# The second tile of a split GELU-multiply: loaded in two transfers of four rows, computed in two steps of four rows

## The chip, the cores and the metric

The kernel runs on one core of a Trainium2 chip. The metric is device time in microseconds of one execution, the median of three runs. The engines that take part are ScalarE (ACT), which computes the GELU and issues most stores, VectorE (DVE), which multiplies, SyncE (SP), which issues all loads and the last stores, and the core's 16 DMA engines, which move the data.

## The reference

```python
x = np.random.randn(32, 512, 2048).astype(np.float32)

def reference(x):
    half_dim = x.shape[-1] // 2
    x1, x2 = x[..., :half_dim], x[..., half_dim:]
    gelu_x1 = 0.5 * x1 * (1 + erf(x1 / np.sqrt(2)))
    return (gelu_x1 * x2).astype(np.float32)
```

The input has 16384 rows of 2048 float32 (134.2 MB); the output has 16384 rows of 1024 (67.1 MB).

## The kernel before

The rows are cut into 16 tiles. A tile is 128 partitions of R = 8 rows each, and the 8 rows of one partition lie next to each other in memory: 64 KB per partition in, 32 KB out, so 8.39 MB in and 4.19 MB out for a tile. There are two input buffers (`x0`, `x1`) and two output buffers (`o0`, `o1`); tile i uses number i % 2 of each.

Nothing is scheduled by a planner. The order on each engine is the order in which the Python loop issues it, and all waits are written by hand:

- `load` (L49) issues a load on SyncE; `store` (L56) lets the issuing engine wait until VectorE has done all multiplies so far (`mul_done`) and then issues the store.
- Before the loop, tile 0 is loaded in two halves of four rows (semaphores `first[0]` and `first[1]`), and tile 1 in one transfer of eight rows (L69; semaphore `ready[1]`). A 4 KB load of scrap is issued on ScalarE.
- In the loop (from L75), each tile is computed in steps. Tiles 0 and 15 take rows (0,2), (2,4), (4,8); all others rows (0,5), (5,8) (L79). A step is a GELU on ScalarE (L87) from the first half of each row into the output buffer, and then a multiply on VectorE (L95) of that with the second half of each row, in place.
- ScalarE waits at a tile's first step for `ready[k]`, which counts both the load of this tile and the store of the tile two before it, whose output buffer it takes over.
- Tile 0 is stored by two half stores on ScalarE; tiles 1 to 13 by one store each on ScalarE; tile 14 by one, and tile 15 by two half stores, on SyncE.
- After tile i, SyncE waits for its last multiply and issues the load of tile i + 2 into the buffer that has come free. So up to two loads can stand in SyncE's DMA ring, and up to two stores in ScalarE's.

At the end ScalarE, VectorE and SyncE clear the semaphores (L119 to L125), and SyncE waits for the last three stores.

Of the kernel before, what the change touches and what calls it, by code (L numbers as in the profile page):

```python
# [1 line left out]

# [4 lines left out]

GELU = mybir.ActivationFunctionType.Gelu


@with_exitstack
def kernel(
    ctx: ExitStack,
    tc: tile.TileContext,
    x: bass.AP,
    out: bass.AP,
):
    nc = tc.nc
    P = nc.NUM_PARTITIONS

    x_flat = x.flatten_outer_dims()
    out_flat = out.flatten_outer_dims()
    n_rows, dim = x_flat.shape
    half = dim // 2

    R = 8
    x_t = x_flat.rearrange("(n p r) d -> n p r d", p=P, r=R)
    o_t = out_flat.rearrange("(n p r) d -> n p r d", p=P, r=R)
    n_tiles = x_t.shape[0]
    x_bufs = [nc.alloc_sbuf_tensor(f"x{k}_tile", [P, R, dim], x.dtype) for k in range(2)]  # L30
    o_bufs = [nc.alloc_sbuf_tensor(f"o{k}_tile", [P, R, half], out.dtype) for k in range(2)]

    first = [nc.alloc_semaphore(f"first{j}") for j in range(2)]
    ready = [nc.alloc_semaphore(f"ready{k}") for k in range(2)]
    gelu_done = nc.alloc_semaphore("gelu_done")
    mul_done = nc.alloc_semaphore("mul_done")
    tail_stored = nc.alloc_semaphore("tail_stored")
    opened = nc.alloc_semaphore("opened")  # L40
    scrap = nc.alloc_sbuf_tensor("scrap_tile", [8, 128], x.dtype)
    n = {sem.name: 0 for sem in [*first, *ready, gelu_done, mul_done, tail_stored, opened]}

    def counted(ins, sem, by):
        ins.then_inc(sem, by)
        n[sem.name] += by

    def load(i, rows, sem):
        ins = nc.sync.dma_start(out=x_bufs[i % 2][:, rows, :], in_=x_t[i][:, rows, :])  # L49
        counted(ins, sem, 16)  # L50
        return ins

    def store(queue, i, rows, sem):
        queue.wait_ge(mul_done, n[mul_done.name])
        counted(
            queue.dma_start(out=o_t[i][:, rows, :], in_=o_bufs[i % 2][:, rows, :]), sem, 16  # L56
        )

    opening = nc.scalar.dma_start(out=scrap[:, :], in_=x_t[0][:8, 0, :128])
    counted(opening, opened, 16)
    for ins in (
        opening,
        load(0, slice(0, 4), first[0]),
        load(0, slice(4, 8), first[1]),
        load(1, slice(0, 8), ready[1]),  # L69
    ):  # L70
        tc.no_tile_sem_insts.add(ins.ins.name)
    tc.close()
    tc.compile()  # L73

    for i in range(n_tiles):  # L75
        k = i % 2
        last = i == n_tiles - 1
        pieces = i == 0 or last
        steps = ((0, 2), (2, 4), (4, 8)) if pieces else ((0, 5), (5, 8))  # L79
        for lo, hi in steps:  # L80
            rows = slice(lo, hi)
            if i == 0 and lo % 4 == 0:
                nc.scalar.wait_ge(first[lo // 4], 16)
            elif lo == 0:
                nc.scalar.wait_ge(ready[k], n[ready[k].name])
            counted(
                nc.scalar.activation(  # L87
                    out=o_bufs[k][:, rows, :], in_=x_bufs[k][:, rows, :half], func=GELU
                ),
                gelu_done,  # L90
                1,
            )
            nc.vector.wait_ge(gelu_done, n[gelu_done.name])
            counted(
                nc.vector.tensor_mul(  # L95
                    out=o_bufs[k][:, rows, :],
                    in0=o_bufs[k][:, rows, :],
                    in1=x_bufs[k][:, rows, half:],
                ),
                mul_done,  # L100
                1,
            )
            if pieces and hi % 4 == 0:
                if last:
                    store(nc.sync, i, slice(hi - 4, hi), tail_stored)
                else:
                    store(nc.scalar, i, slice(hi - 4, hi), ready[k])
        if not pieces:
            if i == n_tiles - 2:
                store(nc.sync, i, slice(0, R), tail_stored)  # L110
            else:
                store(nc.scalar, i, slice(0, R), ready[k])
        if i + 2 < n_tiles:
            nc.sync.wait_ge(mul_done, n[mul_done.name])
            load(i + 2, slice(0, R), ready[k])


    nc.scalar.wait_ge(opened, 16)
    nc.scalar.drain()  # L119
    for sem in (*first, *ready, opened):  # L120
        nc.scalar.sem_clear(sem)
    nc.vector.drain()
    nc.vector.sem_clear(gelu_done)
    nc.sync.sem_clear(mul_done)
    nc.sync.wait_ge(tail_stored, n[tail_stored.name]).then_inc(  # L125
        tail_stored, -n[tail_stored.name]
    )


# [1 line left out]
_INS = ['x']  # L131
_OUTS = [((32, 512, 1024), 'float32')]


# [23 lines left out]
```

## Time and profile before

| what | value |
|---|---|
| time, median of 3 runs | 469.3 us (469.29 to 469.43) |
| span of the profiled execution | 467.8 us |
| VectorE busy | 140.5 us, 34 multiplies |
| ScalarE busy | 115.5 us, 34 GELUs and a table load |
| bytes moved by DMA | 201.34 MB, 430 GB/s over the span |

The span runs from the first to the last instruction of one profiled execution. The profiled execution's own time isn't listed apart from its span; the three runs lie 1.5 us above it, and that much is taken for what lies around the span. In the profile's rows a window's DMA share and GB/s book a packet where it starts, so that short windows go above and below the true rate; long ones are exact.

### The profile page before, as it was taken

The page shows a single profiled execution, that of the slowest core. Times are in us where ns is not written, and L with a number is a line of the kernel's source. Part 1 is how long each engine was busy: PE and PEld are TensorE (multiplying, and loading weights), DVE is VectorE, ACT ScalarE, POOL GpSimd, SP SyncE. Part 2 cuts the span into 40 slices and gives each one's busy share as a digit, 9 for nine tenths or more (in the row PEclk, how much of TensorE's full clock was granted, in tenths as well). Part 3 has the DMA queues.
Part 4 walks back from the last instruction along what each step waited for, and adds up shares of the span by engine and source line. Part 5 has one row for each costly group of instructions (what it writes and reads, how often), then busy time and mean ns, then how long its engine had stood idle before and what let it go on. Part 6 is the DMA issues. An engine that isn't in the chain of part 4 may idle for free.

```text
span 467.8 us, 154 instructions
## 1 busy us (share of the span) xinstructions
DVE 140.5 (30%) x34; ACT 115.5 (25%) x35; POOL 0.2 (0%) x4
## 2 busy tenths in 40 slices
DVE  0330515207051060511606115060150702507043
ACT  1320606041060410604105050050501506014060
POOL 0000000000000000000000000000000000000000
DMA  8999999999999999999999999999999999999988
GB/s 359 448 448 448 398 406 496 403 403 448 459 437 403 440 412 493 403 403 448 487 409 403 445 406 493 403 403 448 493 403 403 448 426 471 403 426 426 493 384 379
DMA packets 5057, 201.34 MB, mean 430 GB/s; under 512 B 568, under 2 KB 576, under 8 KB 576
## 3 DMA queue, kind: packets, MB, share of 16 engines
q1 hardware_dynamic: 2880, 142.61, 70.6%
q10 hardware_dynamic: 2176, 58.73, 29.1%
q14 instruction: 1, 0.01, 0.0%
HBM read 134.22 MB, written 67.11 MB: 430 GB/s over the span
## 4 chain that ended last, share of the span: by engine, by line
DMA 76%; DVE 14%; ACT 8%; ACTq 0%; SPq 0%; issue 0%
DMA out_dram<-o_tile 66%; DVE o_tile L95 14%; DMA x_tile<-in_x_dram 10%; ACT o_tile L87 8%; ACTq L119 0%; SPq L49 0%
## 5 line engine op out<-in xcount | busy, mean ns | idle before, releaser
L95 DVE TENSOR_TENSOR o_tile<-o_tile,x_tile 128x5120 f32<-128x5120 f32 (+3 forms) x34 | 140.5, 4171 | 319.7 <-ACT o_tile L87 319.7
L87 ACT ACTIVATE o_tile<-x_tile 128x5120 f32<-128x5120 f32 (+3 forms) x34 | 114.3, 3407 | 337.3 <-DMA out_dram<-o_tile 301.8
L87 ACT ACT_TABLE_LOAD x1 | 1.3, 1283 | 2.9 <-PEq L73 2.9
L142 POOL MEMSET const-bfloat16-1.0<- 128x1 bf16 x1 | 0.1, 102 | 0.0
L142 POOL MEMSET const-uint8-127<- 128x1 uint8 x1 | 0.1, 101 | 0.0
L142 POOL MEMSET const-float32-0.0<- 128x1 f32 x1 | 0.1, 99 | 0.2 <-issue 0.2
L142 POOL MEMSET const-float32-1.0<- 128x1 f32 x1 | 0.1, 98 | 0.0
## 6 DMA issues: line engine op xcount, KB each, us to landing
out_dram<-o_tile ACTq DMA_DIRECT2D x13, 4096.0 KB, 44.7
x_tile<-in_x_dram SPq DMA_DIRECT2D x2, 4096.0 KB, 16.7
out_dram<-o_tile ACTq DMA_DIRECT2D x2, 2048.0 KB, 34.4
out_dram<-o_tile SPq DMA_DIRECT2D x1, 4096.0 KB, 25.2
out_dram<-o_tile SPq DMA_DIRECT2D x2, 2048.0 KB, 7.8
x_tile<-in_x_dram SPq DMA_DIRECT2D x15, 44.4
scrap_tile<-in_x_dram ACTq DMA_DIRECT2D x1, 4.0 KB
```

Source lines behind the costliest of these rows:

```text
L87: nc.scalar.activation(out=o_bufs[k][:, rows, :], in_=x_bufs[k][:, rows, :half], func=GELU),
L95: nc.vector.tensor_mul(out=o_bufs[k][:, rows, :], in0=o_bufs[k][:, rows, :], in1=x_bufs[k][:, rows, half:],),
L142: nc = _bacc.Bacc("TRN2", target_bir_lowering=False, num_devices=1)
```

## The change

Tile 1 is loaded by two transfers, rows 0 to 4 and rows 4 to 8, each with a semaphore of its own (`ready[1]` and the new `second`). Both stand in SyncE's ring behind the two halves of tile 0, as the one transfer did. Tile 1 is computed in steps (0,4) and (4,8) instead of (0,5) and (5,8); its second GELU waits for `second`. Its store is still one transfer of eight rows after both steps. One more semaphore is cleared at the end. All other tiles are as they were.

```diff
+    second = nc.alloc_semaphore("second")
...
         load(0, slice(4, 8), first[1]),
-        load(1, slice(0, 8), ready[1]),
+        load(1, slice(0, 4), ready[1]),
+        load(1, slice(4, 8), second),
     ):
...
         steps = ((0, 2), (2, 4), (4, 8)) if pieces else ((0, 5), (5, 8))
+        if i == 1:
+            steps = ((0, 4), (4, 8))
         for lo, hi in steps:
             rows = slice(lo, hi)
             if i == 0 and lo % 4 == 0:
                 nc.scalar.wait_ge(first[lo // 4], 16)
+            elif i == 1 and lo == 4:
+                nc.scalar.wait_ge(second, 16)
             elif lo == 0:
                 nc.scalar.wait_ge(ready[k], n[ready[k].name])
...
-    for sem in (*first, *ready, opened):
+    for sem in (*first, *ready, opened, second):
         nc.scalar.sem_clear(sem)
```

More of the change, by code (lines that the diff above doesn't have):

```diff
@@ L40 @@
     opened = nc.alloc_semaphore("opened")
+    second = nc.alloc_semaphore("second")
     scrap = nc.alloc_sbuf_tensor("scrap_tile", [8, 128], x.dtype)
-    n = {sem.name: 0 for sem in [*first, *ready, gelu_done, mul_done, tail_stored, opened]}
+    n = {sem.name: 0 for sem in [*first, *ready, gelu_done, mul_done, tail_stored, opened, second]}
     def counted(ins, sem, by):
```

## The prediction

> **What bounds the kernel now.** I read the page's DMA rows first, because both engines are idle for most of the span (VectorE 30% busy, ScalarE 25%).
>
> ```profile
> span 467.8 us, 154 instructions
> DMA packets 5057, 201.34 MB, mean 430 GB/s; under 512 B 568, under 2 KB 576, under 8 KB 576
> q1 hardware_dynamic: 2880, 142.61, 70.6%
> q10 hardware_dynamic: 2176, 58.73, 29.1%
> ```
>
> q1 is SyncE's ring (all loads, and the stores of tiles 14 and 15), q10 is ScalarE's ring (the other stores). The last column is the time of their packets as a share of 16 DMA engines' span: 70.6 + 29.1 = 99.7%, or 466.4 of 467.8 us. The rest, 1.4 us, is no more than the front: in the packet records the first data packet starts near 2.2 us (neighbouring packets overlap by some ns, so the two don't add up exactly), and from there to the end no engine is without a packet. The stretches of the steady part say the same (columns: length, busy time and count of VectorE, ScalarE, GpSimd, clock, DMA share, GB/s):
>
> ```profile
> 71.40:100.40 29.00, 8.76 (x2) 7.12 (x2) 0.00 (x0) 1.00 1.00 434
> 100.40:129.40 29.00, 8.76 (x2) 7.12 (x2) 0.00 (x0) 1.00 1.00 434
> 129.40:158.40 29.00, 8.76 (x2) 7.13 (x3) 0.00 (x0) 1.00 1.00 434
> ...
> 448.50:458.00 9.50, 6.74 (x3) 7.21 (x3) 0.00 (x0) 1.00 1.01 435
> ```
>
> One tile (8.39 MB in, 4.19 MB out) takes 29.00 us at 434 GB/s with the DMA share at 1.00, and the tail runs at the same rate. So the kernel is bound by bytes through 16 DMA engines. The chain of waits tells a different story, of latencies, and that has to be weighed:
>
> ```profile
> 1.64 45.36 DMA x_tile<-in_x_dram
> ...
> 47.02 4.48 ACT o_tile L87
> ...
> 51.52 8.77 DVE o_tile L95 x2
> ...
> 60.31 40.07 DMA out_dram<-o_tile
> ```
>
> Tile 1 is on it: its load lands at 47.0, GELU and multiply take 13.27 us, its store goes out at 60.31. But that store then takes 40.07 us for 4.19 MB, which alone is 9.7 us of moving at 434 GB/s: it stands in a ring behind other work. A chain through a queued transfer is no proof that starting it earlier ends it earlier.
>
> The timeline around the change and at the tail:
>
> ```profile
> 12.79 3.71 ACT L87 ACTIVATE o_tile<-x_tile 128x2048 f32<-128x2048 f32 x2 [8.65 <-DMA x_tile<-in_x_dram]
> ...
> 22.47 3.62 ACT L87 ACTIVATE o_tile<-x_tile 128x4096 f32<-128x4096 f32 x1 [5.97 <-DMA x_tile<-in_x_dram]
> ...
> 47.02 7.12 ACT L87 ACTIVATE o_tile<-x_tile 128x5120 f32<-128x5120 f32 x2 [20.93 <-DMA x_tile<-in_x_dram]
> ...
> 71.40 7.12 ACT L87 ACTIVATE o_tile<-x_tile 128x5120 f32<-128x5120 f32 x2 [17.26 <-DMA out_dram<-o_tile]
> ```
>
> **How the two rings share.** By packet count a full load is 128 packets of 64 KB, a full store 128 of 32 KB, a half load 128 of 32 KB, a half store 128 of 16 KB. Each engine takes one packet of each ring in turn: tile 1's load lands at 47.0 and tile 0's first half store, a quarter of its bytes but as many packets, at 19.26 + 27.9 = 47.2. So what counts is packets, and the change halves the packets' size in tile 1's load.
>
> **Part 1, two transfers for one (L69).** It removes 128 packets of 64 KB, adds 256 of 32 KB. Median packet times in the records are 2.418 and 1.213 us; with 8 and 16 of them per engine that is 19.34 against 19.41 us, +0.06 us. A second completion packet per engine is 0.009 us. One more issue on SyncE (0.38 to 0.43 us in the chain's SPq rows) delays the barrier ahead of ScalarE's table load by about 0.4 us; that load ends at 4.1 and ScalarE then waits until 12.79, so 8 us cover it. Without that cover it would cost 0.4 us. SyncE has nothing else until 30.5.
>
> The join between the halves is a boundary that the trace doesn't have in tile 1. Its nearest row is the join between tile 0's halves, queued alike: from 12.79 to 22.47 is 9.68 us for 4.19 MB, 433 GB/s, so nothing is lost. Another boundary did lose something: the 16 first packets of tile 1's load, 64 KB behind 32 KB, took 2.42 to 2.87 us, on average 0.25 above the median. After the change that step from 32 to 64 KB stands at tile 2's load, with the store ring empty as before, so I move the 0.25 us rather than strike it out. Bounds: -0.25 if it vanishes, +0.5 if each of two restarts of ScalarE's ring (below) costs as much again.
>
> The Trainium skill speaks against splitting: DMA: Bandwidth & Descriptors, "Anatomy of one DMA — SWDGE (gpsimd) path", fits 2.0 us + bytes/436e3 per DMA, and its "Rules for kernel authors" say to coalesce. By it the sum would be +2.0 us; the fit is for another issue path, and the 9.68 us above show no such term between queued transfers.
>
> **Part 2, where tile 1 lands.** Before, load 1 had 4 parts of 5 of the engines beside store 0's halves. Now it is 32 KB against 16, 2 parts of 3. The first half, with the first half store: 6.29 MB / 434 = 14.5 us, so 22.5 + 14.5 = 37.0. The second half with the second half store (issued at 30.58, in time): 51.5, which is 4.5 us later than 47.0. In exchange store 0 lands at about 51.5, not 71.4. No bytes are gained or lost.
>
> **Part 3, two steps of four rows (L79) and the new wait.** These rows price it:
>
> ```profile
> L95 DVE TENSOR_TENSOR o_tile<-o_tile,x_tile 128x5120 f32<-128x5120 f32 x14 | 76.9, 5493 | 279.5 <-ACT o_tile L87 279.5
> L87 ACT ACTIVATE o_tile<-x_tile 128x5120 f32<-128x5120 f32 x14 | 62.6, 4469 | 300.8 <-DMA out_dram<-o_tile 279.9 <-DMA x_tile<-in_x_dram 20.9
> L95 DVE TENSOR_TENSOR o_tile<-o_tile,x_tile 128x4096 f32<-128x4096 f32 x2 | 8.8, 4424 | 7.7 <-ACT o_tile L87 7.7
> L87 ACT ACTIVATE o_tile<-x_tile 128x4096 f32<-128x4096 f32 x2 | 7.2, 3608 | 6.0 <-DMA x_tile<-in_x_dram 6.0
> ```
>
> The first step runs from 37.0 to 45.1, in idle time of both engines. ScalarE then stands in the new wait until 51.5; behind it are only the second step and store 1's issue. The second step takes 3.61 + 4.42 = 8.03 us, where the tail after the landing was 13.27, so tile 1 is done at 59.6 instead of 60.3. Busy time is the same (8.85 against 8.84 us on VectorE).
>
> **What is late next.** Store 1 and load 3 are issued at 59.6, 0.7 us earlier. Load 2 has had the engines alone since 51.5: 3.5 of its 8.39 MB are in, 4.9 are left at two thirds of 434, so it lands at 76.4 (74.4 if store 1 takes some 4 us to reach the engines; tile 0's first store took 5.5 us from issue to first packet). That is 3 to 5 us later than now (71.1). Tile 2 is done at about 89, store 1 lands at 88.5: the store ring may be dry for a moment, while load 3 moves alone. Load 3 lands near 104 instead of 100.1, and from there each tile takes 29.0 us again. Thus ScalarE starts all middle tiles about 4 us late, and stores land some 13 us ahead of the loads, where now both land within 0.3 us of each other (44.4 and 44.7 us after issue).
>
> At the end the stores run out first. Store 2 starts near 91 and lands near 119, so store 13, eleven tiles later, lands near 438. Load 15 starts near 423 (104 + 11 x 29), shares until 438 (15 us at 289 GB/s, 4.3 MB) and has the engines alone for the other 4.1 MB, 9.4 us: about 448. The bytes agree: at its landing all loads and stores 0 to 13 have moved, 192.9 MB, the same as at 448.5 now. Store 14 stands behind load 15 on SyncE's ring. Then 9.7 us of it cover tile 15's first half (done 6.46 us after its start now: 448.51 to 454.97), and its first half store covers the second half, issued at 460.2 with 14.5 us of stores to move from 448.5 on, that is until 463.0. That leaves 2.8 us, with 1.5 us from an issue to its first packet at the front (0.73 to 2.2). The cover holds, with 1.3 us over.
>
> **Sum.** +0.06 +0.01 + 0 (join) + 0 (steps) + 0 (issue) = +0.07 on the span: 467.9. The times beside it run 1.5 us above the span of the profiled execution (469.3 - 467.8), so the forecast is 469.4.
>
> **Rivals.**
> - Slower, a fixed cost at the join: the engines move nothing between the halves, at 37 us. The first load lands 12.0 us after issue, of which 9.7 are bytes, so 2.3 us is the most that rows allow: 471.6. It decides if the second half's packets start only when the first has landed. Against it: 9.68 us between tile 0's halves.
> - Slower, the late loads are not made good: load 15 lands 4 us late because store 13 doesn't land ahead of it, and the engines go idle earlier on: 473.3. It needs a moment with both rings empty; each load is issued about 13 us after the landing of the one two before it, while the next takes at least 19.3 us, so this has 6 us of room.
> - Faster, the chain of waits is right: tile 1's tail after its landing is 8.03 instead of 13.27 us and that is passed down to the end, 464.1. It needs load 1 to land at 47.0 still and engines that could move more than 434 GB/s; 466.4 us of packets leave no room.
> - The split itself can't fail to be made; it may be hidden altogether, which is my forecast.
>
> **Chances.** Forecast 0.83, fixed cost 0.06, late loads 0.05, chain 0.06. About 0.2% (0.94 us) is what a measurement of this kernel can tell from no change, so the forecast is "same", from 468.4 to 470.2. Its own range: the bounds -0.25 and +0.5, and 0.2 either way for which of the 16 engines ends last (their last packets end between 467.40 and 467.84 now): 468.9 to 470.2. It holds the forecast's 0.83 and needs none of the rivals.
>
> **What would show it.** Right: q1 with 2880 + 128 + 16 = 3024 packets, 434 GB/s in a 29 us stretch, ScalarE's steps of tile 1 at about 37 and 51.5, tile 2 at 74 to 77, middle tiles released by the load and not the store, tile 15 near 448. Wrong: tile 15 starting over 1 us off, a stretch below 430 GB/s, or more than 2 us between the last byte due and the end of the span.

## The result, and the profile after

| | before | changed |
|---|---|---|
| median of 21 runs | 469.31 us (469.15 to 470.04) | 470.40 us (469.52 to 470.92) |
| ratio | | 1.0019, 95% interval 1.0013 to 1.0024 |
| span of the profiled execution | 467.8 us | 468.3 us (that run took 469.66) |

The changed kernel is slower by 0.19%, some 0.9 us (1.09 us between the medians). The forecast was 469.4 in 468.9 to 470.2, so the median lies 0.2 us above the range. The times of the changed kernel aren't one cluster: 10 of 21 runs lie at 469.5 to 469.9, 11 at 470.4 to 470.9, so the median is the lowest run of the upper group. Below, a run at 470.15 or above is called long; before has none among the 21. The profiled execution of the changed kernel is a short one.

The DMA rows of the page, after:

```profile
span 468.3 us, 156 instructions
...
DMA packets 5201, 201.34 MB, mean 430 GB/s; under 512 B 584, under 2 KB 592, under 8 KB 592
...
q1 hardware_dynamic: 3024, 142.61, 70.6%
q10 hardware_dynamic: 2176, 58.73, 29.1%
```

The 3024 packets and the unchanged 99.7% are as forecast: as before, no engine is without a packet between its first and its last. So are the 29 us stretches (length, VectorE, ScalarE, GpSimd, clock, DMA share, GB/s):

```profile
110.00:139.00 29.00, 8.82 (x3) 7.18 (x3) 0.00 (x0) 1.00 1.00 434
```

The timeline at the places of the prediction:

```profile
22.76 3.62 ACT L93 ACTIVATE o_tile<-x_tile 128x4096 f32<-128x4096 f32 x1 [6.26 <-DMA x_tile<-in_x_dram]
...
38.01 3.62 ACT L93 ACTIVATE o_tile<-x_tile 128x4096 f32<-128x4096 f32 x1 [11.64 <-DMA x_tile<-in_x_dram]
...
52.56 3.62 ACT L93 ACTIVATE o_tile<-x_tile 128x4096 f32<-128x4096 f32 x1 [10.93 <-DMA x_tile<-in_x_dram]
...
75.81 7.12 ACT L93 ACTIVATE o_tile<-x_tile 128x5120 f32<-128x5120 f32 x2 [19.63 <-DMA out_dram<-o_tile]
...
104.70 7.12 ACT L93 ACTIVATE o_tile<-x_tile 128x5120 f32<-128x5120 f32 x2 [21.77 <-DMA out_dram<-o_tile]
...
448.92 7.22 ACT L93 ACTIVATE o_tile<-x_tile 128x2048 f32<-128x2048 f32 x3 [18.11 <-DMA out_dram<-o_tile]
```

Tile 1's steps start at 38.0 and 52.6 (forecast 37.0 and 51.5), tile 2 at 75.8, tile 3 at 104.7, and tile 15 is back at 448.9. But the first row is already late: tile 0's second half started at 22.47 before and starts at 22.76 now. That half lies ahead of everything that was changed in its ring. Tile 15 is 0.41 late (448.92 against 448.51), and the span 0.49: what is lost is lost early and kept.

**Where the engines lose it.** The packet records give the start and duration of each packet; a 32 KB packet takes 1.213 us, a 64 KB one 2.418. They don't name the engine, but each packet starts as the one before it on its engine ends, to a few ns, so the 16 engines can be told apart. Their times stand here on the clock of the timeline; a landing shows in the semaphores 0.3 to 0.5 us after the last packet. Summed over the 16 engines and divided by 16, the time above these values between 18 and 60 us is 0.38 us before and 0.82 us after, in the changed kernel nearly all at 20.5 to 26 us: from 1.2 us after tile 0's first half store is issued (19.26) until its packets are going (its first ones start at 23.6 to 24.9). Loads slow down there, up to 2.05 us for 32 KB. Behind 60 us the short run loses 0.02 us more. The second quantity is when each engine finishes: the kernel ends when the last of 16 completion packets is in. Before, they come 0.44 us apart, the last 0.27 us after their mean.

A reading trap in the waits view: it still puts the middle waits down to the store.

```profile
ACT o_tile L93 <- DMA out_dram<-o_tile: 300.2, 14, 22.0
ACT o_tile L93 <- DMA x_tile<-in_x_dram: 36.9, 4, 11.6
```

Load and store count up the same semaphore `ready[k]`, and the view can't tell whose increment came last. The records by ring can: load 5 (SyncE's ring) ends at 161.6 to 162.1, store 3 (ScalarE's ring) at 150.7 to 151.3, and tile 5 starts at 162.7. The load released it.

### The profile page after: what moved, and what is told of

Same layout as the page of the kernel before. It is cut to its first block, busy times and chain, and to the rows that moved or that the text cites. A ratio compares the mean times of both kernels' runs of the same rounds, so it can differ in the third digit from the quotient of the medians.

```text
span 468.3 us, 156 instructions
## 1 busy us (share of the span) xinstructions
DVE 140.6 (30%) x34; ACT 115.7 (25%) x35; POOL 0.2 (0%) x4
## 3 DMA queue, kind: packets, MB, share of 16 engines
q1 hardware_dynamic: 3024, 142.61, 70.6%
## 4 chain that ended last, share of the span: by engine, by line
DMA 74%; DVE 13%; ACT 8%; another core or an unknown queue 2%; ACTq 0%; SPq 0%; issue 0%
DMA out_dram<-o_tile 66%; DVE o_tile L101 13%; ACT o_tile L93 8%; DMA x_tile<-in_x_dram 8%; ACTq L125 0%; SPq L50 0%
```

## The experiments

The theories: O, all of it comes from the opening at 21 to 26 us. R, it comes from 60 to 95 us, where ScalarE's ring has run dry and starts again with store 1; sharpened to J and J2, where what counts is when store 1 joins the loads. T, a gap at the tail. And that the second step or the new wait costs it. All but c4 (one run with a profile) were timed in five rounds beside the kernel before.

**a1, the changed kernel again.**

> The changed kernel once more. Its profile lost 0.45 us against before between 21 and 24 us, where tile 0's first half store joins the loads, and nothing after that; its times lie in two groups, near 469.7 and near 470.7. Theory O (opening): the same place costs 0.4 to 0.5 us in the short group and 1.4 to 1.5 us in the long one. Theory R (restart): the long group's extra 1.0 us stands at 60 to 95 us, where ScalarE's store ring runs dry and starts again. Theory T (tail): it stands after 448 us, with a gap ahead of the last stores. All: median 470.1 to 470.5, two groups.

470.31 us, 9 of 11 runs long, ratio 1.0023 (1.0014 to 1.0032); here the times run from 469.80 to 470.72 without a clear gap. This profile is of a long run:

```profile
span 468.9 us, 156 instructions
...
449.51 7.22 ACT L93 ACTIVATE o_tile<-x_tile 128x2048 f32<-128x2048 f32 x3 [18.02 <-DMA out_dram<-o_tile]
```

The first line is the page's, the second the timeline's. Tile 15 starts 0.59 later than in the short run, with the tail as long as ever (19.4 us): T falls. By the records the engines' mean end is no later than in the short run (467.57 against 467.60), but the last one comes 1.01 us after the mean. At store 1's join 15 engines start its first packet at 66.04 to 66.47 and one at 64.04, a turn earlier (a turn is one packet of each ring that has any; here a 64 KB load packet of 2.418 us). The out-of-step engine then has single slow load packets (0.31, 0.11, 0.06, 0.26 and 0.13 us above 2.418 at 65, 134, 164, 229 and 280 us) and is the one that ends last; a load or store is done only when its last engine is. The first slow packet stands at the join, and three of the other four are this engine's first packet of a new load. O, that the opening is where the extra 1.0 us stands, falls for the long group.

**a2, the load split, the steps of before.**

```diff
-        if i == 1:
-            steps = ((0, 4), (4, 8))
...
-            elif i == 1 and lo == 4:
-                nc.scalar.wait_ge(second, 16)
             elif lo == 0:
                 nc.scalar.wait_ge(ready[k], n[ready[k].name])
+                if i == 1:
+                    nc.scalar.wait_ge(second, 16)
```

> Load 1 split in two as in the changed kernel, but computed in the steps of before, (0,5) and (5,8), once both halves are there. Theory O: the loads and the first half store are as in the changed kernel, so the same times, 469.6 to 470.9 in two groups. Theory R: tile 1 is done 5 us later, so store 1 starts later and ScalarE's ring stays empty longer; the long group is still there. A rival that blames the second step or the new wait: 469.3.

469.55 us, 0 of 11 long, 1.0008 (0.9999 to 1.0017). The interval reaches no change, but the lowest of these 11 runs (469.50) is above the highest of the 33 runs of before beside them (469.43). The opening lost what the changed kernel's did (0.78 us against 0.82), and there are no long runs. Splitting alone gives the short group; something later makes the long one. What differs later is tile 1's steps and, with them, store 1, issued at 65.61 and not at 60.66.

**a3, the steps alone.**

```diff
+        if i == 1:
+            steps = ((0, 4), (4, 8))       # load 1 in one transfer, as before
```

> Load 1 in one transfer as before, but steps (0,4) and (4,8). Theory O: as before, 469.2 to 469.4, one group, since the packets of the opening are those of before. Theory R: as before too, since ScalarE's ring doesn't run dry. The rival that blames the steps: 470.2 to 470.5.

469.35 us, none long, 1.0002 (0.9993 to 1.001), as before. Here the opening lost 0.59 us (before: 0.38), and tile 0's second half starts at 22.57. On the unsplit load the steps cost nothing. The 0.59 against 0.38, with the same opening, is also how far two executions differ there.

**a4, the changed kernel with one store for tile 0.**

```diff
...
-                    store(nc.scalar, i, slice(hi - 4, hi), ready[k])
...
+            elif i == 0 and hi == R:
+                store(nc.scalar, i, slice(0, R), ready[k])
```

> The changed kernel, but tile 0 is stored by one transfer after its last step (issued at about 31 us) and not by two halves. Theory O: no store comes in at 21 to 24 us, so that stretch loses nothing or at most the 0.25 us of a new load's first packets; the loss shows where the one store joins, at 33 to 36 us, beside packets of 32 KB: 0.4 us and two groups there. If it is the boundary from tile 0's load to tile 1's that costs it, the loss stays at 21 to 24 us. Time 469.3 to 470.9 either way; the place tells.

469.81 us, 4 of 11 long, 1.0015 (1.0006 to 1.0024). The place tells: nothing is lost at 18 to 30 us (tile 0's second half starts at 22.59, although the boundary to the split load 1 is there), and 0.95 us at 32 to 36, after the one store's issue at 30.70. So the loads lose it to the store's arrival, not to the boundary of two loads. This profile is of a long run (470.26), again with one engine behind, 0.82 us after the mean.

**b1 and c4, tile 1 stored in halves.**

```diff
+            if i == 1:
+                store(nc.scalar, i, rows, ready[k])
...
-        if not pieces:
+        if not pieces and i != 1:
```

> The changed kernel, but tile 1 is stored in two halves of four rows, each after its step, so that the first stands behind tile 0's second half store and ScalarE's ring is never empty. Theory J (join: the long group comes from store 1 joining an empty ring just as the engines turn from one 64 KB packet to the next, so that one engine takes its first store packet a turn ahead of the other 15 and ends late): no long group, 469.5 to 469.9, all 16 engines' last packets within 0.7 us. Theory O (all of it comes from the opening at 21 to 24 us): two groups as in the changed kernel, median 470.1 to 470.5.

470.00 us, 5 of 12 long, four of them at 472.45 to 474.69, 1.0035 (1.0015 to 1.0055). A miss for J: here store 1 queues behind tile 0's stores and joins nothing, and it is worse. In its profile (469.94) the last engine drifts in small steps, from 0.23 us behind the mean at 54 us to 0.70 at 415. c4 was to catch a run of over 472 us:

> The kernel with tile 1 stored in halves once more, for a profile of its long runs (4 of 12 were at 472.4 to 474.7). If one DMA engine's drift is what makes long runs: the mean of the 16 engines' last packets stays within 0.6 us of before's, and the last engine ends 3 us or more after the mean. If all engines lose: the mean moves by 3 us. In a short run (469.5 to 470.2): mean as in its first profile, the last engine 0.3 to 0.9 us behind the mean.

It took 469.96 us, so it is no such run; the engine that ends last goes from level with the mean at 54 us to 0.56 us behind it at 415. What makes the longest runs stays open.

**b2 and b3, store 1 behind six (b2) or twelve (b3) GELUs on the scrap tile.**

```diff
+        if i == 1:
+            nc.scalar.wait_ge(opened, 16)
+            nc.scalar.wait_ge(mul_done, n[mul_done.name])
+            for j in range(6):
+                nc.scalar.activation(out=pads[j][:, :], in_=scrap[:, :], func=GELU)
```

> The changed kernel, but ScalarE runs six GELUs on the scrap tile between tile 1's last multiply and the issue of store 1, about 1.2 us, half of a 64 KB packet's 2.42 us. Theory J: store 1 reaches the engines amid their packets, all 16 start it in the same turn, no long group, 469.5 to 469.9. Theory O: two groups, median 470.1 to 470.5.

> As the kernel before it, with twelve GELUs, about 2.4 us, a whole packet. Theory J: store 1 reaches the engines one turn later at the same point, so the long group is back (some runs at 470.4 to 470.9). Theory O: two groups too. A delay that is simply good for it, whatever its phase: 469.5 to 469.9.

Both missed as experiments, as b2's timeline shows:

```profile
60.49 0.31 ACT L119 ACTIVATE pad_tile<-scrap_tile 8x128 f32<-8x128 f32 x1 [4.56 <-DVE o_tile L102]
60.66 0.34 ACTq L58 DMA_DIRECT2D out_dram<-o_tile  x1
60.71 1.09 ACT L119 ACTIVATE pad_tile<-scrap_tile 8x128 f32<-8x128 f32 x5
```

The store went out at 60.66, ahead of GELUs that stand before it in the program: its issue doesn't wait for them to run. Both thus issue store 1 as the changed kernel does (b3 at 60.77): b2 470.20 us with 6 of 11 long, b3 469.68 with none. That b3 has none is against any theory by which an issue at 60.4 to 60.8 must give long runs; the experiments with a real delay, below, come back to it. b2's profile is of a long run (span 469.2), and there all 16 engines began store 1 in the same turn, at 66.08 to 66.72; the last one fell behind by five single slow packets, one of 0.21 us at 64 and four, of 0.09 to 0.39, each its first packet of a new load. A sixth slow packet (0.24 us at 415.6) is another engine's and stands beside an 8 KB fetch of instructions by the DMA engines (415.3). So being a turn out of step, as in a1, is one way to lag and not the only one: J falls in that strict form.

**b4, the kernel before, with one store for tile 0.** The same edit as a4's, on the unsplit load.

> The kernel before the change, load 1 in one transfer, but tile 0 stored by one transfer after its last step. The changed kernel with this store lost 0.95 us per engine in slow packets of 32 KB at 33 to 36 us. If the size of the load packets that the first store meets sets that price, this one, which meets 64 KB packets, loses 0.3 to 0.5 us there, as before does at 22 to 25 us, and takes 469.2 to 469.4 us. If the price hangs on the store's own size (32 KB here, 16 KB before) it loses 0.9 us and takes 469.7 to 469.9.

471.05 us, 7 of 11 long, 1.0031 (1.0022 to 1.0041), and 0.98 us lost at 33 to 36 us. Load 1's first 64 KB packets, behind packets of 32 KB, all take 2.418 us here: with no store arriving, that boundary costs nothing. The size of the load packets that the store meets doesn't set the price alone: with the whole store (32 KB packets, issued at 30.6) it is 0.95 to 0.98 beside either load. Four runs lie at 469.75 to 469.85, as the price by the store's size said; the seven at 470.78 to 471.95 were foreseen by neither. They have neither the split load nor the new steps, no profile of one was taken, and their cause is open.

**c1 to c3 and d0 to d3, store 1 really delayed.** Now ScalarE waits for the GELUs by a semaphore before it issues the store: six in c1 and d1, 12 in c2 and d2, 24 in c3 and d3. d0 is the changed kernel.

```diff
...
+            for j in range(6):
+                nc.scalar.activation(
+                    out=pads[j % 12][:, :], in_=scrap[:, :], func=GELU
+                ).then_inc(padded, 1)
...
+            nc.scalar.wait_ge(padded, 6)
```

> In the two kernels with GELUs on the scrap tile the store was issued at 60.7 and 60.8 us, past the running GELUs, so it wasn't late at all. Here ScalarE waits for the last of six such GELUs (a semaphore) before it issues store 1: about 1.3 us later than in the changed kernel, at 61.9. Theory J2 (store 1 joins loads that have the engines alone; what that costs, and whether one engine drops behind, depends on where in the 2.42 us turn of the 64 KB packets it arrives): a share of long runs that differs from the changed kernel's half; none if the arrival is in the middle of a turn: 469.5 to 469.9. Theory O (opening alone decides): two groups, median 470.0 to 470.4, as in the changed kernel.

> The same with twelve GELUs: store 1 about 2.5 us later than in the changed kernel, one whole turn, at 63.1. Theory J2: as the changed kernel, two groups, median 470.0 to 470.4. Theory O: the same. A store 1 that is better the later it comes: fewer long runs than with six.

> The same with 24 GELUs: store 1 about 5 us later, at 65.6, as in the kernel that split the load alone (469.55, no long run among 11). Theory J2: that kernel's times, 469.5 to 469.7, since the time of store 1's issue is what told it from the changed kernel. Theory O and any theory that blames the new wait or the second step: two groups, median 470.0 to 470.4.

c1 469.67, c2 469.82, c3 469.60 us, with 1, 2 and 0 of 11 long. c1 and c3 are as J2 says; c2, a whole turn late, should have had the changed kernel's two groups and a median of 470.0 or more, and didn't. They also had no changed kernel on the same chip beside them. So all four were run on one:

> The changed kernel as control, beside its three delayed forms on the same chip. Theory J2 (the time at which store 1 joins the loads makes the long runs): two groups here too, median 469.9 to 470.5, with 4 of 11 or more at 470.15 or above. If it was the chip: no long runs here, 469.6 to 469.7, like the delayed forms, or as many long runs in those.

> Store 1 issued 1.3 us later, half a turn of the loads' 64 KB packets. J2: at most 2 of 11 runs at 470.15 or above, median 469.6 to 469.75. The chip: as the control.

> Store 1 issued 2.5 us later, a whole turn. J2: between the control and the half turn, median 469.7 to 470.1. The chip: as the control.

> Store 1 issued 5 us later. J2: no run at 470.15 or above, median 469.5 to 469.7. The chip: as the control.

| kernel | store 1 issued at, in its profile | median | range | long runs | ratio (95%) |
|---|---|---|---|---|---|
| d0, changed | 60.40 | 470.38 | 469.54 to 470.94 | 9 of 11 | 1.0022 (1.0013 to 1.0031) |
| d1, half a turn later | 61.85 | 469.71 | 469.59 to 469.88 | 0 of 11 | 1.0008 (0.9999 to 1.0017) |
| d2, a turn later | 63.03 | 469.87 | 469.59 to 470.57 | 2 of 11 | 1.0013 (1.0004 to 1.0022) |
| d3, 5 us later | 65.44 | 469.58 | 469.47 to 470.19 | 1 of 11 | 1.0008 (0.9999 to 1.0017) |

The delay is in d1's timeline, beside d0's (its one line first):

```profile
60.40 0.36 ACTq L57 DMA_DIRECT2D out_dram<-o_tile  x1
...
60.52 1.30 ACT L120 ACTIVATE pad_tile<-scrap_tile 8x128 f32<-8x128 f32 x6 [4.56 <-DVE o_tile L103]
61.85 0.34 ACTq L59 DMA_DIRECT2D out_dram<-o_tile  x1
```

Holding store 1 back by six GELUs (1.3 us), which by itself is a loss, takes 0.67 us off the median. J2 holds in its main point: when store 1 is issued decides how many runs are long. Its forecast for d3, no long run, missed by one (470.19). The new wait and the second step are in all four. The delayed kernels also have GELUs and a semaphore more than d0; b2 has the same six GELUs without the delay and 6 of 11 long runs, so the GELUs alone don't take them away. A kernel with the semaphore and no delay wasn't run.

Whether it is the place in the turn that counts, the packet records can say in part. Store 1's issue is counted here from the mean start of load 2's 16 first packets, in turns of 2.418 us:

| profile | issue, in turns | store 1's first packet on the 16 engines, us | long runs |
|---|---|---|---|
| d0 | 3.60 | 65.93 to 66.40 | 9 of 11 |
| a1 | 3.60 | one 64.04, the others 66.04 to 66.47 | 9 of 11 |
| changed, the first | 3.65 | 66.10 to 66.68 | 11 of 21 |
| b2 | 3.69 | 66.08 to 66.72 | 6 of 11 |
| b3 | 3.75 | 66.20 to 66.85 | 0 of 11 |
| c1 and d1 | 4.13 and 4.18 | 66.07 to 66.68 | 1 and 0 of 11 |
| c2 and d2 | 4.66 and 4.66 | one 66.62 and 66.73, the others 68.45 to 68.81 | 2 and 2 of 11 |
| a2 | 5.73 | 70.89 to 71.39 | 0 of 11 |
| c3 and d3 | 5.78 and 5.74 | 70.69 to 71.36 | 0 and 1 of 11 |

d1's store is issued 1.45 us later than d0's, yet its first packets start at nearly the same time (66.07 to 66.45); so what the delay moved is the issue within the turn. An engine a turn ahead of the others shows at 3.60 in a1 (not in d0) and again, a whole turn on, at 4.66, and in none of the profiles in between. Many long runs came only at 3.60 to 3.69. By that measure b3 lies with a2, c3 and d3, some three quarters into a turn, which have few or none. But c2 and d2 have few too, most kernels have one profile, and two executions of one program differ by 0.05: that the place in the turn is the cause is likely, not shown.

## Why the prediction was wrong, point by point

The two terms, by the packet records of single executions (us; 18 to 60 us for the opening; the mean of the 16 engines' last packets against before's; the last engine against that mean; from the last packet to the end of the span):

```
kernel            span   lost at opening  mean end   last behind mean  to the end
before           467.84       0.38          0            0.27            0.47
a3 steps only    468.10       0.59        +0.19          0.34            0.47
a2 split only    468.29       0.78        +0.46          0.25            0.47
changed, short   468.33       0.82        +0.49          0.36            0.37
changed, long a1 468.95       0.84        +0.46          1.01            0.37
b2, long         469.17       0.72        +0.47          1.23            0.36
```

The last three columns make up the span: for a1 against before, 0.46 + (1.01 - 0.27) - 0.10 = 1.10, and the spans differ by 1.11. In these profiles the mean end moves with the split, and the lag of the last engine is what sets the long runs apart.

- **Part 1, the packets (+0.07) and the join (0): right.** 3024 packets, and between the halves' steps 52.56 - 38.01 = 14.55 us for 6.29 MB, 432 GB/s. The fixed cost per transfer, the first rival, doesn't show at the join that it was priced for. By the fit of the Trainium skill (DMA: Bandwidth & Descriptors, "Anatomy of one DMA — SWDGE (gpsimd) path"), which is for transfers that GpSimd issues, one transfer more would have been 2.0 us; these transfers queued on SyncE's ring show no such term. The rule to coalesce of the Trainium skill (same page, "Rules for kernel authors"), which the prediction sets beside it, is for many small transfers and didn't bear on halves of 4.19 MB.
- **Part 1, "I move the 0.25 us rather than strike it out": wrong, the first mis-sized term.** I saw that load 1's first packets were slow and took it for a matter of the step from 32 to 64 KB packets. a4 shows that it moves with the first store, and b4 that the step from 32 to 64 KB costs nothing without one. And it grew: in 14 profiles with the load split the loads lost 0.54 to 0.92 us at the opening, in the two with the load whole and half stores 0.38 and 0.59, so the two overlap by one profile. That is the short group's part, +0.34 to +0.49 us on the mean end in the changed kernel. My bound of +0.5 held it, by luck: I had put it on restarts of ScalarE's ring, and the one restart, at store 1, cost the engines 0.02 us on average in the short run. Why the first store slows the loads, and most of the time those of 32 KB packets more, is open.
- **Parts 2 and 3, shares, landings, steps: right**, with tile 1's two steps about 1 us late. Store 0's halves now land with load 1's halves, tile 2 starts at 75.8, the stores lead the loads by 11 us, and tile 15 is back at 448.9. Neither the late loads nor the chain of waits showed up at the end.
- **"0.2 either way for which of the 16 engines ends last": wrong, the second mis-sized term, and the one that carried the median out of the range.** It was read off the spread of one execution of before, as if every execution had the same one. The last engine ends 0.03 to 0.09 us further behind the mean in the changed kernel's short runs (d0 and the first profile), and 0.74 and 0.96 in two long ones (a1 and b2), where 0.2 was allowed. What I had in hand was the condition: I wrote that the store ring runs dry and restarts near 60 us, and priced it as the same loss for all engines. It can be a loss for one, and then the others' time doesn't show it. In a1 and b2 the lagging engine's slow packets stand at the join and then, all but one, at its first packet of a new load; why they are slow there, no run here tells.
- The range itself: the bounds +0.5 and 0.2 on 469.4 make 470.1, not 470.2. The measured medians (470.40, and 470.31 and 470.38 in a1 and d0) lie above both.
- The Trainium skill states (same page, "Why a DMA increments its semaphore by 16 and not by 1") that the engines of a transfer finish independently and that only the full count means landed. The traces agree with the first: the kernel's last 16 completions come 0.44 to 1.47 us apart. The second no run here tests.
- Around the span I took 1.5 us; the changed kernel's profiled run shows 469.66 - 468.33 = 1.33, and the runs of before that are listed with their span show the same (469.22 against 467.9). The 1.5 came from setting one execution's span beside other executions' times. That made the forecast too high by some 0.15, so it isn't behind the miss.
- Packet times of the prediction (2.2 us, 467.40 to 467.84) stand 0.47 us later than on the timeline's clock: the first data packet starts at 1.74, the engines end at 466.93 to 467.38, and the cover of 1.3 us at the tail was 1.8. No term of the sum hangs on it.

## What to carry to other kernels

In this kernel the DMA engines are full from the first packet to the last, and there a change of steps alone moved nothing (a3, 1.0002). What was left to lose lay where transfers of two rings meet. The first store to join the loads cost each engine 0.38 to 0.98 us. A later store, into a ring that had run dry, cost the average engine 0.05 us or less (0.2 in b3), but can leave one engine behind to the end. So look in the changed kernel for the places where a ring runs dry and refills, and try that transfer a little later; keeping the ring filled is no cure by itself (b1 was worse). When medians differ by less than one engine's lag, look at the list of times before the mean: two groups ask for a profile of each.

## What the runs showed that was not expected

- The end of this kernel, bound by DMA, is the end of its slowest engine: two executions of one program with nearly the same mean end (467.60 and 467.57 us) differ by 0.62 us in span.
- ScalarE's DMA issue passes its own GELUs that are still to run (store at 60.66, five of the six GELUs after it); a wait for a semaphore that they count up holds it back (61.85, in d1).
- Two rings take turns by whole packets, here of up to 64 KB, so halving the rows of a transfer changes its share of the engines: load 1 and a half store took 4 : 1 of the bytes before and 2 : 1 after.
